# Three split fp32r passes for the transform matmuls of a long convolution, and a filter spectrum read once

## The chip, the cores and the metric

The kernel runs on one core of one Trainium2 chip. The metric is the device time of one execution in microseconds, lower is better. The core has a TensorE (PE, with its weight loads shown apart as PEld), a VectorE (DVE), a ScalarE (ACT), a GpSimd (POOL) and a SyncE (SP), which here issues nearly all of the DMAs. Each engine works through its own queue of instructions in order.

## The reference, cut to what matters

One encoder layer of 2048 positions by 1024 channels: a combined input projection, a Hyena group (512 channels, two gated long convolutions) beside an mLSTM group, an output projection, cross-attention, a squared-ReLU MLP and norms. The change touches the long convolution only:

```python
for o, gate in enumerate((g1, g2)):
    conv = irfft(rfft(z, n=2 * L) * spec[:, o], n=2 * L)[:, :L]
    z = gate * (conv + z * skip[o])
```

The spectrum `spec` is that of an implicit filter: a small sine network over position features, times a decay window, transformed in the same way. All inputs and outputs are fp32.

## The kernel before

**The transforms.** A transform of length 4096 over 2048 points is done as two matmul stages with constant matrices. The first stage multiplies slabs of 128x512 with the two 128x128 matrices `f1` (parity p = 0, 1); its result goes to DRAM and comes back regrouped; the second stage multiplies with one of 32 matrices `dm`. The inverse uses `em` and then `e2` in the same way. All of these are plain fp32 matmuls of 128x128 by 128x512.

**`filters`** (L158) makes the spectrum. For each of 16 slabs j and both orders o, it multiplies the hidden layer with `w3` (L253, L254), takes the window (DVE, L256 and L257), forms the sum (DVE, L261) and the difference (POOL, L262) of the forward and the backward part, and runs `front` (L238), which is the two `f1` matmuls, evicted by ScalarE (L239) into staging tiles that go to DRAM. A helper `late` holds back each `front` until the instructions of the next slab have been emitted. After that come 32 blocks of `dm` matmuls (L284), whose result is the spectrum `hd` in DRAM.

**`hyena`** (L627) has three stages for each order o. Stage one: per slab one load and two `f1` matmuls (L709), evicted by ScalarE and VectorE in turn (L140, L142). Middle stage, 16 steps: `load2` (L654) fetches `dm`, `em`, the regrouped slab `t` and the spectrum's real and imaginary rows `hr`, `hi`, each of them twice, once for partitions 0 to 63 and once for 64 to 127 (L664, L665); then for each of two halves the `dm` matmul (L723), two 64x512 instructions on ScalarE that swap the halves (L725, L726), a product on VectorE (L727), a product on POOL (L728), a sum on VectorE (L729), and, held back by one half, the `em` matmul (L691) with its eviction (L692) and the store `zg` (L694). Last stage: per slab two accumulating `e2` matmuls for each of two halves (L742) and the gate product (L743).

**The projection beside it.** `sweep` and `natural` (L495, L592) do the input projection. They already work with split operands: a helper writes a rounded high part in fp32r (ScalarE) and the rest as a low part (VectorE), and `mm3` (L294) runs three fp32r matmuls, high by high, high by low and low by high (L295 to L297).

**The order of the work.** `weave` interleaves `filters`, then `hyena`, with the projection's generators by the costs that they yield; the pools give the number of buffers (`a`: slabs of 128x1024, `b`: tiles of 128x512, and four PSUM banks under each of the tags `hy` and `mm`). Within what the program's order and the buffers allow, the framework orders the instructions of each engine by a modelled timeline, so a change in one place moves instructions on all engines.

In time, the span runs through `filters` with the projection (to about 470 us), `hyena` with the projection (to about 1130 us), then memory projection, mLSTM, output projection, attention and the MLP, which hold the rest.

Of the kernel before, what the change touches and what calls it, by code (L numbers as in the profile page):

```python
# [20 lines left out]
CH = 512  # L21
# [76 lines left out]
class Prog:  # L98
# [22 lines left out]
    def mm(self):  # L121
        return self.ps.tile([128, 512], F32, tag="mm", name="mm", bufs=4)
# [35 lines left out]
    def filters(self):  # L158
# [1 line left out]
        sd = [self.dram(f"fs{o}", (2, 128, 16, CH)) for o in range(2)]  # L160
        hd = self.dram("hd", (2, 32, 128, CH))
        with tc.tile_pool(name="f_sb", bufs=1, side="right") as sb:
            def ta(bufs=7):
                return sb.tile([128, 2, CH], F32, tag="a", name="a", bufs=bufs)

            def tb(bufs=8):
                return sb.tile([128, CH], F32, tag="b", name="b", bufs=bufs)

            w1 = sb.tile([66, 128], F32, name="w1")
            w2 = sb.tile([128, 128], F32, name="w2")  # L170
            w3 = sb.tile([128, 2, CH], F32, name="w3")
            f1 = sb.tile([128, 2, 128], F32, name="f1")
            nc.vector.memset(w1, 0.0)
            nc.vector.memset(w2, 0.0)
            nc.gpsimd.dma_start(out=w1[0:33, 0:64], in_=a["hy_filt_w1"][0])
# [8 lines left out]
            w3v = a["hy_filt_w3"][0].rearrange("k (o r c) -> r k o c", o=2, r=2)  # L184
            for h in range(2):
                nc.gpsimd.dma_start(out=w3[64 * h:64 * h + 64], in_=w3v[h])
            nc.gpsimd.dma_start(out=f1, in_=a["c_f1"])

            def sine(dst, src, b, fr):
                u, k = tb(), tb()  # L190
# [44 lines left out]
            def front(e, st, jj, o, js):  # L235
                for p in range(2):
                    pp = self.hy()
                    nc.tensor.matmul(pp, f1[:, p], e[p], start=True, stop=True)  # L238
                    nc.scalar.copy(st[p][:, jj], pp)  # L239
                    if jj == 1:  # L240
                        nc.sync.dma_start(out=sd[o][p, :, js], in_=st[p])

            nxt = windows(0)
            for j2 in range(8):
                js = slice(2 * j2, 2 * j2 + 2)
                yield 14
                (wf, wb), nxt = nxt, windows(j2 + 1)
                for o in range(2):
                    st = [ta() for p in range(2)]
                    for jj in range(2):  # L250
                        j = 2 * j2 + jj
                        pf, pb = self.hy(), self.hy()
                        nc.tensor.matmul(pf, hid[0:64, j::16], w3[0:64, o], start=True, stop=True)  # L253
                        nc.tensor.matmul(pb, hid[64:128, j::16], w3[64:128, o], start=True, stop=True)  # L254
                        f, b = tb(), tb()
                        nc.vector.tensor_tensor(f, pf, wf[:, jj], ALU.mult)  # L256
                        nc.vector.tensor_tensor(b, pb, wb[:, jj], ALU.mult)  # L257
                        if j == 0:
                            nc.vector.tensor_tensor(f[0:1], f[0:1], (skip, skip2)[o][0:1], ALU.add)
                        e = [tb() for p in range(2)]  # L260
                        nc.vector.tensor_tensor(e[0], f, b, ALU.add)  # L261
                        nc.gpsimd.tensor_tensor(e[1], f, b, ALU.subtract)  # L262
                        late(lambda e=e, st=st, jj=jj, o=o, js=js: front(e, st, jj, o, js))
            late(None)
            def blocks(o, i):
# [27 lines left out]
    def mm3(self, ps, lh, ll, rh, rl, start, stop):  # L293
        mm = self.nc.tensor.matmul  # L294
        mm(ps, lh, rh, start=start, stop=False)  # L295
        mm(ps, lh, rl, start=False, stop=False)  # L296
        mm(ps, ll, rh, start=False, stop=stop)  # L297

    def split(self, hi, lo, src):
        self.nc.scalar.copy(hi, src)  # L300
# [326 lines left out]
    def hyena(self, es):  # L627
# [7 lines left out]
        sb = es.enter_context(tc.tile_pool(name="h_sb", bufs=1, side="right"))  # L635

        def ta():
            return sb.tile([128, 2, CH], F32, tag="a", name="a", bufs=10)

        def tb():  # L640
            return sb.tile([128, CH], F32, tag="b", name="b", bufs=5)

        f1 = sb.tile([128, 2, 128], F32, name="f1")
        e2 = sb.tile([128, 2, 128], F32, name="e2")
        nc.sync.dma_start(out=f1, in_=a["c_f1"])
        nc.sync.dma_start(out=e2, in_=a["c_e2"])
        ghy = self.bcast(sb, a["hy_norm_g"], CH, "ghy")
        def load1(o, j2):
            z = ta()
# [4 lines left out]
        def load2(o, i):  # L654
            p, k = divmod(2 * i, 16)
            dm = sb.tile([128, 2, 128], F32, tag="dm", name="dm", bufs=2)
            em = sb.tile([128, 2, 128], F32, tag="em", name="em", bufs=2)
            nc.sync.dma_start(out=dm, in_=a["c_dm"][:, 2 * i:2 * i + 2])
            nc.sync.dma_start(out=em, in_=a["c_em"][:, 2 * i:2 * i + 2])
            t, hr, hi = ta(), ta(), ta()  # L660
            nc.sync.dma_start(out=t, in_=sds[o][p, 8 * k:8 * k + 16].rearrange("(k r) j c -> (r j) k c", k=2))
            src = hd[o, 2 * i:2 * i + 2].rearrange("k (r l) c -> r l k c", r=2)
            for h in range(2):
                nc.sync.dma_start(out=hr[64 * h:64 * h + 64], in_=src[0])  # L664
                nc.sync.dma_start(out=hi[64 * h:64 * h + 64], in_=src[1])  # L665
            if i == 0:
                nc.sync.dma_start(out=hr[64:65, 0], in_=hd[o, 0, 64:65])
                nc.vector.memset(hi[0:1, 0], 0.0)
                nc.vector.memset(hi[64:65, 0], 0.0)  # L669
            return dm, em, t, hr, hi  # L670
# [25 lines left out]
        for o in range(2):  # L696
            sd, gd = sds[o], gds[o]
            q = [load1(o, 0), load1(o, 1)]
            for j2 in range(8):
                yield 3.5  # L700
                js = slice(2 * j2, 2 * j2 + 2)
                z = q.pop(0)
                if j2 < 6:
                    q.append(load1(o, j2 + 2))
                st = [ta() for p in range(2)]
                for jj in range(2):
                    for p in range(2):
                        pp = self.hy()
                        nc.tensor.matmul(pp, f1[:, p], z[:, jj], start=True, stop=True)  # L709
                        self.copy(st[p][:, jj], pp)  # L710
                for p in range(2):
                    nc.sync.dma_start(out=sd[p, :, js], in_=st[p])
            nxt = load2(o, 0)
            for i in range(16):
                yield 3.5
                p, k = divmod(2 * i, 16)
                dm, em, t, hr, hi = nxt
                if i < 15:
                    nxt = load2(o, i + 1)
                gs = ta()  # L720
                for m in range(2):
                    pp = self.hy()
                    nc.tensor.matmul(pp, dm[:, m], t[:, m], start=True, stop=True)  # L723
                    xt, y = tb(), tb()
                    nc.scalar.activation(xt[0:64], pp[64:128], AF.Copy, scale=-1.0)  # L725
                    nc.scalar.copy(xt[64:128], pp[0:64])  # L726
                    nc.vector.tensor_tensor(y, pp, hr[:, m], ALU.mult)  # L727
                    nc.gpsimd.tensor_tensor(xt, xt, hi[:, m], ALU.mult)  # L728
                    nc.vector.tensor_tensor(y, y, xt, ALU.add)  # L729
                    late(lambda m=m, em=em, y=y, gs=gs, dst=gd[p, 8 * k:8 * k + 16]: back(m, em, y, gs, dst))  # L730
            late(None)
            nxt = load3(o, 0)
            for j2 in range(8):
                yield 3.5
                js = slice(2 * j2, 2 * j2 + 2)
                r, gate = nxt
                if j2 < 7:
                    nxt = load3(o, j2 + 1)
                for jj in range(2):
                    pp = self.hy()  # L740
                    for p in range(2):
                        nc.tensor.matmul(pp, e2[:, p], r[p][:, jj], start=p == 0, stop=p == 1)  # L742
# [922 lines left out]
```

## Time and profile before

| | |
|---|---|
| time, median of 3 runs | 3452.99 us (3443.19 to 3454.02) |
| time of the profiled execution | 3453.44 us |
| its span (first to last instruction) | 3451.7 us |
| mean granted clock of TensorE | 0.971 |
| TensorE busy | 3220.7 us (93%) |
| VectorE, ScalarE, GpSimd busy | 2116.4, 1256.9, 1274.5 us |
| DMA, mean over the span | 208 GB/s |

The profile is of one execution. Busy time of TensorE is modelled and pipelined: a matmul's recorded duration overlaps that of the next one, so throughput is read from start to start. A plain fp32 matmul leaves two records, an fp32r matmul one. An idle time is put down to the engine or DMA that released the waiting instruction.

### The profile page before, as it was taken

How to read it: one execution, taken by the hardware profiler on the slowest of the kernel's cores; microseconds unless marked ns; L12 is line 12 of the kernel's file. 1: busy time of each engine (PE TensorE's matmuls, PEld its weight loads, DVE VectorE, ACT ScalarE, POOL GpSimd, SP SyncE). 2: the span in 40 equal slices, each digit the busy share in tenths (PEclk: the TensorE clock that was granted, in tenths of full speed). 3: DMA queues.
4: the chain of work that ended last, by engine and by line, in shares of the span. 5: the costliest groups of instructions: out<-in, count | busy, mean ns of one | idle time of the engine just before them, and what ended most of it. 6: DMA issues, size and time to landing. Idle time of an engine off the chain costs nothing. (4 is left out here: it accounts for less than half of the span.)

```text
span 3451.7 us, 46201 instructions
## 1 busy us (share of the span) xinstructions
PE 3220.7 (93%) x15671; PEld 2574.5 (75%) x15671; DVE 2116.4 (61%) x3831; ACT 1256.9 (36%) x2410; POOL 1274.5 (37%) x902
## 2 busy tenths in 40 slices
PE   6999999999999888699998998999999988999997
PEld 5656666676666878598988896778788867888876
DVE  7585235434547667666865344888977734555695
ACT  4344435623553334323333333222322233333335
POOL 2131002200123212233334114776765577344483
PEclk9999999999999989799999999999999999999999
DMA  5356879987898589767767546665644465344434
GB/s 163 115 202 212 295 270 261 289 316 246 226 246 292 152 269 296 226 226 260 242 248 257 208 170 205 208 198 165 205 164 147 144 217 179 120 149 135 133 96 156
DMA packets 477704, 716.98 MB, mean 208 GB/s; under 512 B 41258, under 2 KB 259440, under 8 KB 468252
## 3 DMA queue, kind: packets, MB, share of 16 engines
q1 hardware_dynamic: 475864, 711.16, 64.4%
q0 software_dynamic: 1600, 2.86, 0.4%
q8 instruction: 124, 2.03, 0.2%
q14 instruction: 112, 0.92, 0.1%
q10 hardware_dynamic: 4, 0.00, 0.0%
HBM read 486.31 MB, written 227.57 MB: 207 GB/s over the span
## 5 line engine op out<-in xcount | busy, mean ns | idle before, releaser
L1273 DVE TENSOR_TENSOR bl<-wr,bh 128x512 fp32r<-128x512 f32 x213 | 229.0, 1079 | 201.6 <-ACT bh L1272 198.7
L295 PE MATMUL mm<-xh,wh 128*128 128x512 f32 (+1 forms) x768 | 316.8, 413 | 12.1 <-ACT P L531 7.1
L296 PE MATMUL mm<-xl,wh 128*128 128x512 f32 (+1 forms) x768 | 303.1, 395 | 0.3 <-DVE xr_y L150 0.2
L297 PE MATMUL mm<-xh,wl 128*128 128x512 f32 (+1 forms) x768 | 302.9, 395 | 0.6 <-DVE wl L301 0.6
L728 POOL TENSOR_TENSOR b<-b,a 128x512 f32<-128x512 f32 x64 | 90.3, 1412 | 497.0 <-DVE a L669 226.3
L1272 ACT CAST ah<-w 128x512 fp32r<-128x512 f32 x190 | 117.0, 622 | 380.5 <-PE mm L296 162.9
L301 DVE TENSOR_TENSOR wl<-wn,wh 128x512 fp32r<-128x512 f32 (+1 forms) x224 | 164.4, 762 | 137.2 <-ACT wh L300 136.6
L1272 ACT CAST bh<-wr 128x512 fp32r<-128x512 f32 x232 | 143.7, 620 | 272.6 <-PE mm L297 196.8
L297 PE MATMUL mm<-bh,al 128*128 128x512 f32 x576 | 222.6, 397 | 20.9 <-POOL al L1273 18.7
L295 PE MATMUL mm<-bh,ah 128*128 128x512 f32 x576 | 228.7, 397 | 7.4 <-ACT ah L1272 7.4
L296 PE MATMUL mm<-bl,ah 128*128 128x512 f32 x576 | 227.4, 395 | 0.0
L1273 DVE TENSOR_TENSOR al<-w,ah 128x512 fp32r<-128x512 f32 x190 | 188.5, 993 | 32.5 <-ACT ah L1272 32.1
L297 PE MATMUL mm<-act,wl 128*128 128x512 f32 x512 | 202.8, 399 | 4.1 <-DMA wl<-vw 4.1
L295 PE MATMUL mm<-act,wh 128*128 128x512 f32 x512 | 201.8, 398 | 2.5 <-DMA wh<-vw 2.5
L296 PE MATMUL mm<-act,wh 128*128 128x512 f32 x512 | 202.7, 396 | 0.0
L300 ACT CAST wh<-wn 128x512 fp32r<-128x512 f32 (+1 forms) x224 | 130.3, 619 | 192.7 <-PE mm L296 75.3
L295 PEld LDWEIGHTS mm<-xh,wh 128*128 128x128 f32 x768 | 148.8, 194 | 60.9 <-issue 18.2
L1141 POOL TENSOR_TENSOR ssum<-ssum,sq 128x512 f32<-128x512 f32 x56 | 75.8, 1354 | 309.7 <-ACT sq L1140 305.2
L296 PEld LDWEIGHTS mm<-xl,wh 128*128 128x128 f32 x768 | 148.8, 194 | 45.2 <-issue 19.5
L297 PEld LDWEIGHTS mm<-xh,wl 128*128 128x128 f32 x768 | 148.6, 193 | 42.9 <-issue 15.8
L295 PE MATMUL hy<-bh,ah 128*128 128x512 f32 x448 | 175.5, 392 | 3.0 <-DVE acc L1544 3.0
L296 PE MATMUL hy<-bl,ah 128*128 128x512 f32 x448 | 174.6, 390 | 0.0
(371 smaller groups left out, 9094.2 us busy)
## 6 DMA issues: line engine op xcount, KB each, us to landing
wr<-hc SPq DMA_DIRECT2D x224, 256.0 KB
a<-hd SPq DMA_DIRECT2D x128, 256.0 KB
w<-in_ff_w_dram SPq DMA_DIRECT2D x128, 256.0 KB
hc<-t SPq DMA_DIRECT2D x128, 256.0 KB
wn<-in_w_in_dram SPq DMA_DIRECT2D x104, 256.0 KB
hc<-q SPq DMA_DIRECT2D x96, 256.0 KB
fs<-a SPq DMA_DIRECT2D x32, 512.0 KB
a<-fs SPq DMA_DIRECT2D x32, 512.0 KB
```

Source lines behind the costliest of these rows:

```text
L295: mm(ps, lh, rh, start=start, stop=False)
L296: mm(ps, lh, rl, start=False, stop=False)
L297: mm(ps, ll, rh, start=False, stop=stop)
L300: self.nc.scalar.copy(hi, src)
L301: self.nc.vector.tensor_tensor(lo, src, hi.bitcast(F32), ALU.subtract)
L728: nc.gpsimd.tensor_tensor(xt, xt, hi[:, m], ALU.mult)
L1141: nc.gpsimd.tensor_tensor(ssum, ssum, sq, ALU.add)
L1272: self.nc.scalar.copy(hi, src)
L1273: eng.tensor_tensor(lo, src, hi.bitcast(F32), ALU.subtract)
```

## The change

Three matmul groups, those at L238 (`front`), L709 and L742, become three split passes each with `mm3`. Their constant matrices are split once into a high and a low part; the moving tiles are split where they are used by a new helper `halved`: a cast on ScalarE and a subtraction on VectorE or POOL. The matmuls with `dm`, `em`, `w1`, `w2` and `w3` stay plain fp32. In `load2`, each spectrum row is loaded once, into one half of the partitions, and copied to the other half by ScalarE. The pools change: in `filters` `a` from 7 to 6 buffers and `b` from 8 to 10, in `hyena` `a` from 10 to 9 and `b` from 5 to 7.

```diff
@@ filters
-                nc.tensor.matmul(pp, f1[:, p], e[p], start=True, stop=True)
+                self.mm3(pp, f1[0][:, p], f1[1][:, p], *e[p], True, True)
...
                         nc.vector.tensor_tensor(e[0], f, b, ALU.add)
                         nc.gpsimd.tensor_tensor(e[1], f, b, ALU.subtract)
+                        e = [self.halved(sb, e[p], (nc.vector, nc.gpsimd)[p], tag="b", name="b", bufs=10) for p in range(2)]
@@ new helper
+    def halved(self, pool, src, eng, **kw):
+        hi, lo = (pool.tile(list(src.shape), F32R, **(kw or {"name": n})) for n in ("ch", "cl"))
+        self.nc.scalar.copy(hi, src)
+        eng.tensor_tensor(lo, src, hi.bitcast(F32), ALU.subtract)
+        return hi, lo
@@ hyena, load2
-            for h in range(2):
-                nc.sync.dma_start(out=hr[64 * h:64 * h + 64], in_=src[0])
-                nc.sync.dma_start(out=hi[64 * h:64 * h + 64], in_=src[1])
+            nc.sync.dma_start(out=hr[0:64], in_=src[0])
+            nc.sync.dma_start(out=hi[64:128], in_=src[1])
+            nc.scalar.copy(hr[64:128], hr[0:64])
+            nc.scalar.copy(hi[0:64], hi[64:128])
@@ hyena, stage one
+                    zh, zl = self.halved(sb, z[:, jj], nc.vector, tag="b", name="b", bufs=7)
                     for p in range(2):
                         pp = self.hy()
-                        nc.tensor.matmul(pp, f1[:, p], z[:, jj], start=True, stop=True)
+                        self.mm3(pp, f1[0][:, p], f1[1][:, p], zh, zl, True, True)
@@ hyena, last stage
-                        nc.tensor.matmul(pp, e2[:, p], r[p][:, jj], start=p == 0, stop=p == 1)
+                        rh, rl = self.halved(sb, r[p][:, jj], (nc.vector, nc.gpsimd)[p], tag="b", name="b", bufs=7)
+                        self.mm3(pp, e2[0][:, p], e2[1][:, p], rh, rl, p == 0, p == 1)
```

More of the change, by code (lines that the diff above doesn't have):

```diff
@@ L162, in filters, with ta, tb @@
         with tc.tile_pool(name="f_sb", bufs=1, side="right") as sb:
-            def ta(bufs=7):
+            def ta(bufs=6):
                 return sb.tile([128, 2, CH], F32, tag="a", name="a", bufs=bufs)
-            def tb(bufs=8):
+            def tb(bufs=10):
                 return sb.tile([128, CH], F32, tag="b", name="b", bufs=bufs)
@@ L171, in filters @@
             w3 = sb.tile([128, 2, CH], F32, name="w3")
-            f1 = sb.tile([128, 2, 128], F32, name="f1")
             nc.vector.memset(w1, 0.0)
@@ L186, in filters @@
                 nc.gpsimd.dma_start(out=w3[64 * h:64 * h + 64], in_=w3v[h])
-            nc.gpsimd.dma_start(out=f1, in_=a["c_f1"])
+            t = tb()[:, 0:256].rearrange("p (a b) -> p a b", a=2)
+            nc.gpsimd.dma_start(out=t, in_=a["c_f1"])
+            f1 = self.halved(sb, t, nc.vector)
             def sine(dst, src, b, fr):
@@ L637, in ta @@
         def ta():
-            return sb.tile([128, 2, CH], F32, tag="a", name="a", bufs=10)
+            return sb.tile([128, 2, CH], F32, tag="a", name="a", bufs=9)
         def tb():
[L641 to L646, printed above, removed]
+            return sb.tile([128, CH], F32, tag="b", name="b", bufs=7)
+        consts = []
+        for n in ("c_f1", "c_e2"):
+            t = ta()[:, 0, 0:256].rearrange("p (a b) -> p a b", a=2)
+            nc.sync.dma_start(out=t, in_=a[n])
+            h, l = (sb.tile([128, 2, 128], F32R, name=n + x) for x in "hl")
+            nc.scalar.copy(h, t)
+            nc.vector.tensor_tensor(l, t, h.bitcast(F32), ALU.subtract)
+            consts.append((h, l))
+        f1, e2 = consts
         ghy = self.bcast(sb, a["hy_norm_g"], CH, "ghy")
```

## The prediction

> **What bounds the kernel now.** First I read the page's busy line, then busy time by stretch, cut where the convolution's stages change. A stretch row gives its length, then busy time of PE, PEld, DVE, ACT and POOL, the granted clock, DMA share and GB/s.
>
> ```profile
> PE 3220.7 (93%) x15671; PEld 2574.5 (75%) x15671; DVE 2116.4 (61%) x3831; ACT 1256.9 (36%) x2410; POOL 1274.5 (37%) x902
> ...
> 105.00:310.00 205.00, 203.18 (x711) 119.09 (x710) 143.22 (x283) 81.88 (x155) 58.48 (x32) 1.00 0.49 168
> 310.00:470.00 160.00, 157.69 (x628) 109.45 (x627) 41.19 (x59) 69.15 (x118) 0.59 (x1) 1.00 0.85 282
> 470.00:550.00 80.00, 77.13 (x299) 51.06 (x299) 30.25 (x49) 29.21 (x47) 4.27 (x3) 1.00 0.80 254
> 550.00:720.00 170.00, 159.10 (x691) 113.80 (x690) 90.80 (x157) 97.55 (x163) 38.73 (x30) 0.98 1.01 283
> 720.00:850.00 130.00, 126.66 (x717) 94.86 (x715) 46.07 (x110) 34.68 (x78) 0.00 (x0) 1.00 0.78 288
> 850.00:1050.00 200.00, 183.84 (x706) 126.53 (x707) 104.75 (x170) 105.91 (x174) 46.01 (x31) 0.97 0.93 242
> 1050.00:1130.00 80.00, 77.41 (x386) 57.63 (x385) 64.09 (x152) 21.37 (x39) 30.41 (x20) 0.98 0.83 278
> ```
>
> TensorE is the bound nearly everywhere: 203 of 205 us in the filters' first part, and 281 of 290 us in the three stretches that hold most of hyena's stage one and last stage (470–550, 720–850, 1050–1130). Only the two middle stretches are looser: PE leaves 11 and 16 us, 27 in all, while the DMA share is 1.01 and 0.93. So fewer TensorE cycles are worth having there, if nothing new holds TensorE up. What holds it today in hyena, and what the middle stage's other engines wait for:
>
> ```profile
> PE hy L691 <- DVE b L729: 9.4, 5, 3.3
> PE mm L295 <- ACT P L531: 4.2, 1, 4.2
> PE hy L691 <- ACT P L531: 3.8, 1, 3.8
> PE hy L723 <- DMA a<-zs: 3.5, 3, 2.3
> ...
> L727 DVE TENSOR_TENSOR b<-hy,a 128x512 f32<-128x512 f32 x64 | 44.1, 688 | 80.4 <-ACT b L726 40.5 <-DMA a<-hd 29.9 <-ACT a L692 5.4
> L728 POOL TENSOR_TENSOR b<-b,a 128x512 f32<-128x512 f32 x64 | 90.3, 1412 | 497.0 <-DVE a L669 226.3 <-ACT b L726 197.0 <-DMA a<-hd 39.0
> ```
>
> The largest wait is for the middle stage's chain, which ends in the sum L729, and that chain is itself late because the spectrum (`hd`) lands late: 29.9 us of waiting on DVE, 39.0 on POOL.
>
> **The matmuls.** Durations overlap, so I count from start to start.
>
> ```profile
> 1033.75 0.39 PE L296 MATMUL mm<-xl,wh 128*128 128x512 f32 x1
> ...
> 1037.23 0.39 PE L296 MATMUL mm<-xl,wh 128*128 128x512 f32 x1
> 1037.46 1.02 PE L691 MATMUL hy<-b,em 128*128 128x512 f32 x2
> 1038.32 1.02 PE L723 MATMUL hy<-a,dm 128*128 128x512 f32 x2
> ...
> L238 PE MATMUL hy<-b,f 128*128 128x512 f32 x128 | 64.4, 607 | 0.2 <-DVE ms L408 0.2
> L709 PE MATMUL hy<-a,f 128*128 128x512 f32 x128 | 61.0, 593 | 1.7 <-DMA a<-hy 1.7
> L742 PE MATMUL hy<-a,e 128*128 128x512 f32 x128 | 59.4, 592 | 0.0
> ```
>
> Fifteen split passes, each with weights of its own, lie between 1033.75 and 1037.23: 0.232 us a pass, 0.70 for three. One plain fp32 matmul of this shape takes 1037.46 to 1038.32, 0.86 us, in two records. Each of the three lines has 128 records, so 64 matmuls: 192 x (0.86 - 0.70) = 31 us of TensorE come off, 10 at L238 and 10.5 each at L709 and L742. By recorded durations it would be a loss (three of 0.39 against two of 0.59 is a wash); I take the starts, since those are what the next instruction sees.
>
> [...]
>
> **Hyena's stage one and last stage.** They add 32 + 64 splits: a cast on ScalarE and a subtraction each, 64 of these on DVE and 32 on POOL. Nearest rows:
>
> ```profile
> L300 ACT CAST wh<-wn 128x512 fp32r<-128x512 f32 x56 | 31.9, 617 | 52.1 <-DMA wn<-in_w_in_dram 36.8 <-PE mm L296 9.8 <-PE mm L297 5.3
> L301 DVE TENSOR_TENSOR wl<-wn,wh 128x512 fp32r<-128x512 f32 x53 | 36.3, 714 | 51.8 <-ACT wh L300 51.8
> L1273 POOL TENSOR_TENSOR al<-wr,ah 128x512 fp32r<-128x512 f32 x52 | 70.5, 1361 | 97.7 <-ACT ah L1272 92.0 <-issue 5.7
> ```
>
> ACT 96 x 0.62 = 59 us, DVE 64 x 0.71 = 46, POOL 32 x 1.36 = 44. The three stretches have 290 us, of which ACT works 85, DVE 140 and POOL 35, and the slabs are loaded one or two ahead, so the splits lie beside TensorE's work. Uncovered, one split ahead of its matmul would cost 0.62 + 0.71 (DVE) to 1.36 us (POOL). Of 21 us I take 18 as won (PE is busy 97% there).
>
> **Filters.** They add 64 splits: ACT 40 us on 82 of 205, DVE 32 subtractions on 143, POOL 32 on 58. Totals fit, so the question is the chain.
>
> ```profile
> 195.81 0.80 PE L253 MATMUL hy<-w,hid 64*128 64x512 f32 x1
> ...
> 198.89 0.80 PE L253 MATMUL hy<-w,hid 64*128 64x512 f32 x1
> ...
> L256 DVE TENSOR_TENSOR b<-hy,a 128x512 f32<-128x512 f32 x32 | 22.0, 686 | 22.2 <-PE hy L253 12.7 <-PE hy L254 9.2
> L262 POOL TENSOR_TENSOR b<-b 128x512 f32<-128x512 f32 x32 | 58.5, 1828 | 223.1 <-DVE b L257 186.8 <-DVE xr_y L155 8.7 <-DVE xr_t L153 8.0
> ```
>
> Where slabs follow each other with no projection between them, one takes 3.08 us (195.81 to 198.89). From the `w3` matmuls to `front` lie two window products (2 x 0.69) and POOL's difference (1.83): 3.2 us. After the change the POOL half adds a cast (0.62) and a second POOL instruction (1.83): 5.7 us. `late` puts one `front` (2 x 0.70) and one pair of `w3` matmuls (1.36, that is 3.08 less two fp32 matmuls of 0.86) between; the loop over two slabs then takes 5.7 + 1.4 + 1.36 = 8.5, 4.2 per slab in place of 3.1. So a slab without projection work beside it loses 1.1 us, and one with it wins its share of 10 us. All 32 dense: 35 lost. I take a third, 11 slabs, as in such runs: 12 lost, 10 won, **+2 us**; bounds -10 and +25. Staging in 6 buffers in place of 7 makes an eviction wait for the store of the slab before; that is inside these bounds.
>
> **The middle stage.** Half of the spectrum's loads go, and 64 copies of 64x1024 come to ScalarE. The spectrum's share of the traffic, over 550 to 700 us:
>
> ```profile
> DMA packets 29598, 43.01 MB, mean 287 GB/s; under 512 B 2737, under 2 KB 14608, under 8 KB 29589
> ...
> a<-hd SPq DMA_DIRECT2D x54, 256.0 KB
> ...
> L726 ACT COPY b<-hy 64x512 f32<-64x512 f32 x64 | 37.0, 578 | 0.8
> L545 ACT ACTIVATE cv<-P,cb,cw 128x1040 f32<-128x1040 f32 x12 | 15.1, 1256 | 0.4
> ```
>
> 54 x 0.256 = 13.8 of 43.0 MB; half is 6.9 MB, 16% of the traffic at a share of 1.01, and two issues fewer per step on SP. For the copy the trace shows no row; a crossing copy of half the width takes 0.58 (L726) and a full-width instruction of 1040 elements 1.26, so 0.58 to 1.26; I take 1.15, near the row of equal length. 64 x 1.15 = 74 us raise ACT from 203 to 277 of the 370 us. ScalarE is in order: in the changed build the pair stands in most steps straight ahead of the half-swap of the next half, and behind a copy that waits for its load are queued that swap, the evictions L692 and the projection's PSUM copies, for which TensorE waits (4.2 and 3.8 us above). DMA relief is worth at most TensorE's 27 idle us; exposed copies at most 74. I take **-7**: the waits for `hd` shrink, and a part is given back.
>
> Small edits cost nothing that can be seen: the three constants are split once, beside the projection's matmuls, under 5 us if uncovered (three casts and subtractions of less than 0.62 + 0.71). At step 0 of each order the one-row load into `hr` now waits for ScalarE's copy, and SP's later loads stand behind it: twice a copy, 2.5 us at most, and loads run a step ahead.
>
> **Sum**: -18 + 2 - 7 = -23 us. The profiled execution took 3453.44 us (span 3451.7 and 1.7 around it), 0.45 above the median of the runs; 3453.4 - 23 = 3430 us. About 0.3%, 10 us, is what a measurement of this kernel can tell from no change. What follows after 1130 us keeps its work; its instructions are reordered in places, for which I leave some us in the range.
>
> **Rivals.**
> - *Relief pays too* (0.17): all 31 us are kept and 18 of the 27 idle us go: 3404. For it: share 1.01 and the waits for `hd`. Against it: ACT at 75%.
> - *The filters' chain eats it* (0.18): every slab is exposed, +35 - 10 = +25 cancels -18 - 7: 3453. For it: DVE at 143 of 205, and POOL's instruction takes 1.83 there against 1.36 elsewhere, so the two engines already slow each other and now both get 32 more. Against it: PE is busy 203 of 205 us there, so projection passes lie between most slabs. [...]
> - *ScalarE holds up the middle stage* (0.23): half of the 74 us stays uncovered, because the copies and their wait for the load stand ahead of the half-swap: -18 + 2 + 37 = +21, 3474, slower. It beats the gain from 16 us, 0.5 us a step over 32 steps, and shows from 0.8. For it: L691 already waits for this chain, and a late load, which today stops DVE or POOL, would stop ScalarE. Against it: fewer bytes land sooner, and TensorE has projection passes between.
>
> **How the numbers follow.** The forecast has 0.42, by itself 3418 to 3443. Faster by over 0.3%: forecast and relief, 0.59. Within: 0.18. Slower: 0.23. The range, 3400 to 3476, takes in the rivals' values and leaves out full exposure of the copies and full relief.
>
> **What would show it.** Per triple of the new matmuls 0.70 from start to start; less than 3 us between the splits and their matmuls as PE idle in 470–550 and 720–850; the end of the last stage near 1107 in place of 1130. In the middle stage, DMA share near 0.85 and waits for `hd` on ACT under 20 us; a PE idle time over 40 us there, released by ACT or L729, means the third rival. In the filters, PE idle before `front` released by POOL above 25 us means the second. A triple at 0.86 or more would refute the whole saving.

## The result and the profile after

| | before | after |
|---|---|---|
| time, median of 4 runs each | 3453.51 us (3443.19 to 3454.84) | 3473.47 us (3470.0 to 3475.6) |
| ratio after to before, 95% interval | | 1.0065 [1.0049, 1.0081] |
| time and span of the profiled execution | 3453.44, 3451.7 us | 3474.58, 3472.9 us |
| mean granted clock of TensorE | 0.971 | 0.964 |
| first and last `dm` matmul of the filters start at | 313.5, 459.7 us | 349.0, 486.9 us |
| last `em` matmul of the middle stage starts at | 1056.8 us | 1084.7 us |

The kernel became 20 us slower, where 23 us faster was forecast. The page's busy line, of the kernel after:

```profile
PE 3229.6 (93%) x15863; PEld 2622.7 (76%) x15863; DVE 2200.2 (63%) x3930; ACT 1399.9 (40%) x2628; POOL 1359.8 (39%) x966
```

TensorE's modelled busy time is 9 us longer, although it has 31 us less to do by start-to-start prices. So here instructions took longer each, or were held inside what is counted as busy. The stretch rows of the kernel after, cut at its own stage ends (length; busy time of PE, PEld, DVE, ACT, POOL; granted clock, DMA share, GB/s), say where:

```profile
105.00:350.00 245.00, 238.33 (x836) 151.67 (x835) 178.31 (x317) 118.26 (x223) 101.13 (x64) 0.91 0.42 144
350.00:480.00 130.00, 128.27 (x502) 87.00 (x500) 32.30 (x48) 58.57 (x101) 0.00 (x0) 1.00 0.95 321
480.00:580.00 100.00, 94.98 (x414) 74.48 (x413) 50.50 (x78) 54.00 (x86) 3.13 (x3) 0.97 0.67 218
580.00:750.00 170.00, 154.77 (x684) 111.70 (x683) 85.88 (x153) 123.63 (x190) 40.45 (x30) 0.98 0.81 237
...
870.00:1090.00 220.00, 204.02 (x810) 144.44 (x809) 114.06 (x194) 144.97 (x219) 42.47 (x32) 0.98 0.68 193
1090.00:1190.00 100.00, 85.56 (x575) 78.48 (x574) 93.36 (x183) 40.38 (x78) 55.52 (x37) 0.97 0.67 222
```

The filters' first part took 205 us before (105 to 310, granted clock 1.00) and takes 245 now, at a clock of 0.91. From there on the delay of 27 us of the last filter `dm` matmul is carried along (28 us at the last `em`). The middle stage (580 to 750 and 870 to 1090) has the load relief: DMA shares of 0.81 and 0.68 where 1.01 and 0.93 stood. The last row is hyena's last stage in the second order: VectorE works 93 of 100 us and TensorE 86, where TensorE worked 77 of 80.

**What happens in the filters.** The same kernel in slices of 5 us, columns as above:

```profile
180.00:185.00 5.00, 4.76 (x27) 3.33 (x26) 5.00 (x6) 4.58 (x9) 3.23 (x2) 1.00 0.44 127
185.00:190.00 5.00, 2.78 (x7) 0.98 (x6) 5.00 (x13) 4.80 (x13) 1.28 (x2) 1.00 0.61 238
190.00:195.00 5.00, 4.97 (x8) 1.83 (x8) 4.98 (x21) 1.73 (x4) 2.90 (x2) 0.53 0.66 230
195.00:200.00 5.00, 5.00 (x8) 2.17 (x8) 5.00 (x12) 1.49 (x3) 1.26 (x1) 0.50 0.09 34
200.00:205.00 5.00, 5.00 (x17) 3.27 (x16) 3.70 (x6) 2.71 (x5) 3.07 (x2) 0.61 0.32 126
...
235.00:240.00 5.00, 4.37 (x8) 1.62 (x7) 5.00 (x17) 1.50 (x3) 2.94 (x2) 0.81 0.26 105
240.00:245.00 5.00, 4.54 (x15) 3.46 (x15) 5.00 (x10) 2.43 (x5) 2.31 (x3) 0.51 0.11 13
...
265.00:270.00 5.00, 3.21 (x7) 1.40 (x7) 3.31 (x7) 4.23 (x12) 2.33 (x2) 0.88 0.20 57
270.00:275.00 5.00, 5.00 (x9) 2.00 (x9) 5.00 (x17) 2.10 (x4) 2.37 (x3) 0.50 0.53 211
...
285.00:290.00 5.00, 5.00 (x15) 2.85 (x14) 2.08 (x3) 2.28 (x4) 0.00 (x0) 0.50 0.50 174
```

Read two columns together. In 185 to 190 TensorE is busy 2.78 of 5 us; in the next ten microseconds it counts as busy throughout, at half the clock. The same follows the gap at 265, and, with less idle time ahead of it, it happens at 235. Cut into slices of half a microsecond and less, the same view puts the half clock at 190.3 to 203.9, 238.1 to 244.9 and 268.8 to 292.7 us: 13.7, 6.8 and 23.9 us. A busy digit of 9 hides most of this; only the clock column shows it. The timeline of all engines over that first gap (start, duration, then what waited and for whom), same kernel:

```profile
186.59 1.87 DVE L309 TENSOR_TENSOR xl<-mm,xh 128x512 fp32r<-128x512 f32 x3
...
186.72 1.23 PE L255 MATMUL hy<-w,hid 64*128 64x512 f32 x2 [0.32 <-DVE b L258]
...
188.47 0.68 DVE L262 TENSOR_TENSOR b<-b 128x512 f32<-128x512 f32 x1
...
189.18 1.14 ACT L303 CAST b<-b 128x512 fp32r<-128x512 f32 x2 [0.20 <-DVE b L262]
...
189.85 1.31 PE L297 MATMUL hy<-b,ch 128*128 128x512 f32 x2 [1.90 <-ACT b L303]
190.19 0.69 DVE L304 TENSOR_TENSOR b<-b 128x512 fp32r<-128x512 f32 x1
...
190.96 0.77 PE L298 MATMUL hy<-b,ch 128*128 128x512 f32 x1
191.53 0.63 PE L299 MATMUL hy<-b,cl 128*128 128x512 f32 x1
192.09 2.07 PE L254 MATMUL hy<-w,hid 64*128 64x512 f32 x2
```

The chain is one of three engines, on queues that have other work: VectorE's sum (L262) stands behind three of the projection's own subtractions (L309), ScalarE's cast (L303) waits 0.20 us for the sum, TensorE waits 1.90 us for the cast, and then the clock is gone: the pair of `w3` matmuls takes 2.07 us where it took 1.23.

Counted in sum: the last filter `dm` matmul is 27 us late although the stage was relieved of 10 us, so 37 us were lost; by then both kernels have done the same work of the projection (283 split triples before, 285 after). The clock accounts for 0.09 x 245 = 22 of them. Of the other 15 the busy rows show 5 as idle time (238.33 of 245 busy, against 203.18 of 205); where the last 10 lie isn't shown.

The saving per triple is there where the clock is full (1.00 from 261.5 to 263). The middle pass (L298) of two triples that follow each other, kernel after:

```profile
261.91 0.39 PE L298 MATMUL hy<-b,ch 128*128 128x512 f32 x1
...
262.61 0.39 PE L298 MATMUL hy<-b,ch 128*128 128x512 f32 x1
```

0.70 us from start to start, as forecast.

### The profile page after: what moved, and what is told of

Its sections match the earlier page's. It is cut to its first block, busy times and chain, and to the rows that moved or that the text cites. A ratio compares the mean times of both kernels' runs of the same rounds, so it can differ in the third digit from the quotient of the medians.

```text
span 3472.9 us, 46975 instructions
## 1 busy us (share of the span) xinstructions
PE 3229.6 (93%) x15863; PEld 2622.7 (76%) x15863; DVE 2200.2 (63%) x3930; ACT 1399.9 (40%) x2628; POOL 1359.8 (39%) x966
## 3 DMA queue, kind: packets, MB, share of 16 engines
q0 software_dynamic: 1600, 2.86, 0.4%
## 5 line engine op out<-in xcount | busy, mean ns | idle before, releaser
L297 PE MATMUL mm<-xh,wh 128*128 128x512 f32 (+1 forms) x768 | 307.8, 402 | 22.6 <-DVE st L142 9.2
L298 PE MATMUL mm<-xl,wh 128*128 128x512 f32 (+1 forms) x768 | 304.9, 397 | 0.0
L298 PE MATMUL mm<-bl,ah 128*128 128x512 f32 x576 | 228.1, 396 | 0.0
L309 DVE TENSOR_TENSOR wl<-wn,wh 128x512 fp32r<-128x512 f32 (+1 forms) x224 | 171.7, 795 | 84.6 <-ACT wh L308 84.0
L298 PE MATMUL mm<-act,wh 128*128 128x512 f32 x512 | 202.9, 396 | 0.0
L298 PEld LDWEIGHTS mm<-xl,wh 128*128 128x128 f32 x768 | 150.1, 195 | 41.7 <-issue 15.6
L298 PE MATMUL hy<-bl,ah 128*128 128x512 f32 x448 | 175.8, 393 | 0.0
```

The lines of the kernel that those rows point to most:

```text
L309: self.nc.vector.tensor_tensor(lo, src, hi.bitcast(F32), ALU.subtract)
```

## The experiments

Ratios are to the kernel before, run beside each group of experiments on the same chip; its median moved between 3443 and 3451 us from group to group, so ratios are compared, not times. "Filters alone" and the like mean the kernel before with that one edit.

| label | what it is | median us | ratio [95%] |
|---|---|---|---|
| e1_filters_as_before | after, filters as before | 3452.64 | 1.0006 [0.9994, 1.0019] |
| e2_filters_alone | filters alone | 3483.06 | 1.0091 [1.0068, 1.0113] |
| e3_load_alone | `load2` alone | 3453.14 | 1.0010 [0.9997, 1.0024] |
| e4_stages_alone | split stage one and last stage alone | 3453.99 | 1.0014 [0.9996, 1.0032] |
| e5_low_on_vector | e2, both low parts on VectorE | 3469.29 | 1.0055 [1.0038, 1.0073] |
| e6_no_low | e2 without the low parts | 3442.07 | 0.9959 [0.9943, 0.9976] |
| e7_no_low_8_tiles | e6 with 8 `b` tiles | 3438.56 | 0.9966 [0.9953, 0.9980] |
| e8_last_stage_plain_in_second_order | e4, last stage of the second order plain | 3446.33 | 0.9990 [0.9975, 1.0005] |
| e9_both_loads_and_copies | all loads kept, copies added | 3474.36 | 1.0062 [1.0042, 1.0081] |
| e10_filters_with_filler | e2 with idle TensorE work added | 3469.84 | 1.0051 [1.0031, 1.0072] |
| e11_stages_less_last_with_load | e8 and `load2` | 3441.26 | 0.9966 [0.9950, 0.9982] |
| e12_stage_one_alone | split stage one alone | 3446.92 | 0.9992 [0.9975, 1.0010] |
| e13_load_copies_on_gpsimd | e3, copies on GpSimd | 3428.17 | 0.9956 [0.9943, 0.9969] |
| e14_e11_copies_on_gpsimd | e11, copies on GpSimd | 3415.79 | 0.9923 [0.9895, 0.9951] |
| e15_e11_copies_on_vector | e11, copies on VectorE | 3416.44 | 0.9923 [0.9899, 0.9948] |
| e16_load_copies_on_vector | e3, copies on VectorE | 3419.65 | 0.9935 [0.9914, 0.9956] |

### The three parts, each by itself

The first four take the change apart: `filters` as before and all else as after (e1), and each part on the kernel before (e2, e3, e4). No other line is edited, and the pools go with their part.

> The changed kernel with the filters' part put back as it was before (plain fp32 front, 7 and 8 buffers); hyena's three edits stay. Theory F (the filters' longer chain costs about 38 us, from TensorE work counted start to start: 68 us lost between 105 and 350 us against 30 between 105 and 310 before): 3473 less 28 (38 lost there less 10 saved), about 3440 to 3447, faster than before. Theory S (ScalarE's copies, which wait 79 us for the spectrum's load, hold up the middle stage): stays at 3465 or above, since the middle stage is unchanged.

> The kernel before with the filters' edit alone. Theory F: 3453 + 28 = about 3480, slower than the whole change. Theory S: 3443, the 10 us of saved TensorE time, or no change.

> The kernel before with load2's edit alone (each spectrum row loaded once and copied by ScalarE), buffers as before. Theory F: within 8 us of 3453 either way, since TensorE lost 45 us in the two middle stretches of the changed kernel and 43 before. Theory S: 3475 to 3490, the waits of the copies reach TensorE.

> The kernel before with the split passes of hyena's stage one and last stage alone (9 and 7 buffers), loads as before. Prediction's term: 3453 - 18 = 3435. Rival (the last stage of the second order becomes bound by VectorE, 93 of 100 us busy in the changed kernel): 3445 to 3450, most of the 21 us given back.

The filters alone cost 0.91%, 31 us; without them nothing is lost (1.0006). e2 and e3 came where theory F had them; e1 came 6 us above its range and e4 4 us above its rival's, each far from the other theory. Neither of the other two parts brings anything: the 21 us of TensorE time that leave stage one and the last stage come to nothing, and so does the relief from half of the spectrum's traffic. The filters' loss is the one seen in the kernel after; e2's row for the same stretch:

```profile
105.00:350.00 245.00, 238.35 (x838) 151.77 (x836) 178.49 (x317) 118.00 (x223) 101.25 (x64) 0.91 0.42 144
```

Same busy times, same clock of 0.91, with the load and the stages left as before. Beside the other parts the filters' edit costs 20 us (after against e1) and alone 31; why some 10 us are won back there wasn't settled.

### The filters: casts, subtractions, slots or the clock

Four edits on top of e2. In e5 GpSimd's subtraction goes to VectorE. Theory P, here and in the two runs after it, is that GpSimd's second instruction, in series behind its difference, makes the chain long (for e5: 3455 to 3465):

```diff
-  e = [self.halved(sb, e[p], (nc.vector, nc.gpsimd)[p], tag="b", name="b", bufs=10) for p in range(2)]
+  e = [self.halved(sb, e[p], nc.vector, tag="b", name="b", bufs=10) for p in range(2)]
```

> The kernel before with the filters' edit alone, but both low parts subtracted by VectorE, so that GpSimd has one instruction per slab again. Measured for the edit as it is: 3483, 33 over the kernel before. [...] Theory D (VectorE is the tight engine there, some 80% busy in 150 to 250 us): slower still, 3490. Theory T (tile slots hold the chain): no change, about 3483.

In e6 the casts stay and the subtractions go; the pass with the low part takes the high part again, so that TensorE's work is unchanged and the correction for the moving operand is left out. e7 is the same with 8 `b` tiles in place of 10.

```diff
-  e = [self.halved(sb, e[p], (nc.vector, nc.gpsimd)[p], tag="b", name="b", bufs=10) for p in range(2)]
+  for p in range(2):
+      hi = sb.tile([128, CH], F32R, tag="b", name="b", bufs=10)
+      nc.scalar.copy(hi, e[p])
+      e[p] = hi, hi
```

> The filters' edit alone without the low part of the moving tiles: the second pass takes the high part again, so the result misses that correction; three passes, casts on ScalarE, no subtraction, six tile slots used per slab in place of eight. Theories P and D (the subtractions): below 3450, about 3443, the saved TensorE time. Theory A (ScalarE's casts in the chain): stays above 3465.

> As the run without the low part (same work left out), but with 8 slots in the pool for six tiles per slab, as tight as 10 for eight. Theory T (tile slots hold the chain): above 3465, most of the loss is back. Theories P and D: as without the low part, within 8 us of it.

Without the subtractions, but with all the casts, the edit is a gain of 0.41% (0.34% with 8 tiles): 14 and 12 us, the forecast's 10 us of saved TensorE time and a little more. In the filters themselves less than that shows: the first filter `dm` matmul starts at 309.3 and 307.7 us, against 313.5 before (349.2 in e2); where the rest was won isn't shown. So the casts cost nothing that counts, and the slots neither. The subtractions cost 0.91 + 0.41 = 1.3%, 45 us, between e2 and e6. With the second one on VectorE (e5) 0.36% comes back, 12 us. None of the three theories was met: P had two thirds of the loss coming back, D had it growing, T had no change. So the loss isn't GpSimd's slow instruction alone. What came back is clock: 0.96 over 105 to 350 us where e2 has 0.91, 12 us of full-speed time. What the instructions take in the kernel after, from the groups by line (busy, mean ns | idle before, releaser):

```profile
L263 POOL TENSOR_TENSOR b<-b 128x512 f32<-128x512 f32 x32 | 56.4, 1764 | 154.4 <-DVE b L258 141.3 <-DVE xr_y L155 5.7 <-DVE P L534 2.3
...
L304 POOL TENSOR_TENSOR b<-b 128x512 fp32r<-128x512 f32 x32 | 44.8, 1399 | 65.7 <-ACT b L303 65.7
...
L303 ACT CAST b<-b 128x512 fp32r<-128x512 f32 x64 | 39.1, 621 | 43.4 <-DVE b L262 31.3 <-POOL b L263 5.1 <-DVE P L534 3.6
...
L262 DVE TENSOR_TENSOR b<-b 128x512 f32<-128x512 f32 x32 | 31.2, 976 | 0.4
...
L304 DVE TENSOR_TENSOR b<-b 128x512 fp32r<-128x512 f32 x32 | 25.1, 784 | 16.6 <-ACT b L303 15.3 <-POOL b L263 1.2
```

The casts wait for VectorE's sum (31.3 us) far more than for GpSimd's difference (5.1): VectorE is the late one. Its sum has no idle time before it (0.4) because other work always stands ahead of it. And it takes longer than before, 0.98 us on the mean in place of 0.79. Single slabs show why (timeline of the kernel after):

```profile
192.28 1.26 POOL L263 TENSOR_TENSOR b<-b 128x512 f32<-128x512 f32 x1 [0.25 <-DVE xr_t L153]
192.30 1.78 DVE L262 TENSOR_TENSOR b<-b 128x512 f32<-128x512 f32 x1
...
301.15 0.69 DVE L262 TENSOR_TENSOR b<-b 128x512 f32<-128x512 f32 x1
301.19 1.80 POOL L263 TENSOR_TENSOR b<-b 128x512 f32<-128x512 f32 x1 [3.96 <-DVE b L258]
```

In 14 of the 32 slabs the sum starts first; it then takes 0.68 to 0.80 us, and the difference 1.73 to 1.81. In ten the difference starts first and the sum ends 0.55 us after it, which makes it 1.13 to 1.81 us long; in the other eight the sum is short (0.67 to 0.79). So one holds up the other. The kernel before has three long sums, and e5, where GpSimd has no subtraction, has four.

How much of the loss is the clock was asked with e10: four extra passes of 256 columns ahead of each triple, whose result the triple overwrites. In its trace such a pass takes 0.119 us from start to start (the median), so this is 64 x 4 x 0.119 = 30 us of work, where 33 had been reckoned.

```diff
   for p in range(2):
       pp = self.hy()
+      for _ in range(4):
+          nc.tensor.matmul(pp[:, 0:256], f1[0][:, p], warm, start=True, stop=True)
       self.mm3(pp, f1[0][:, p], f1[1][:, p], *e[p], True, True)
```

> The kernel before with the filters' edit alone, and four extra passes of 256 columns ahead of each triple of front, whose result the triple overwrites: 64 x 4 x 0.127 = 33 us more TensorE work, which can run while TensorE waits for the splits and keeps it busy. The filters' edit alone measured 3483, and its granted clock fell to 0.76 to 0.91 between 150 and 300 us. Theory C (the fall of the clock after such waits makes most of the loss): clock back to 0.97 or more there, and no slower than 3483, down to 3465. Theory W (the waits themselves make the loss, the clock little): 3490 to 3515.

30 us more work and 0.40%, 14 us, less time than e2, as theory C had it; the first filter `dm` matmul starts at 335.8 us, 13 us earlier than in e2. Beside e2's row above, the same stretch of e10:

```profile
105.00:350.00 245.00, 239.01 (x1102) 172.24 (x1101) 181.81 (x317) 121.47 (x228) 99.92 (x64) 0.97 0.46 161
```

and of e6, which has no subtractions:

```profile
105.00:350.00 245.00, 237.52 (x953) 160.41 (x952) 153.31 (x299) 134.62 (x251) 55.34 (x32) 0.99 0.57 195
```

The clock is 0.97 with the filler and 0.99 without the subtractions, against 0.91: 15 and 20 us of full-speed time over 245. The filler is done in time that the chain would have left empty, and the clock stays at 0.97. That the chain comes first and the clock's fall adds to it is shown by e6 and e10 together; how the 14 us divide isn't shown, since the filler also shifts the order of other work.

### The load: two large effects that cancel

e9 keeps all four loads of a step and adds the two ScalarE copies, which then rewrite what was loaded:

```diff
             for h in range(2):
                 nc.sync.dma_start(out=hr[64 * h:64 * h + 64], in_=src[0])
                 nc.sync.dma_start(out=hi[64 * h:64 * h + 64], in_=src[1])
+            nc.scalar.copy(hr[64:128], hr[0:64])
+            nc.scalar.copy(hi[0:64], hi[64:128])
```

> The kernel before, with both loads of each spectrum row kept and ScalarE's copies added on top (they write the same values again): the price of the copies without the relief of the loads. The load edit alone measured 3453 against 3450. Theory N (both are worth nothing, TensorE is not held up by either): 3450 to 3456. Theory X (the two cancel): the copies alone cost 10 to 30, 3460 to 3480.

The copies alone cost 0.62%, 21 us, and the missing loads give 0.52%, 18 us, back (e3 against e9). This is not quite the copies' price in the change: in e9 a copy also waits for the load that it overwrites, 100 us in all for the first of each pair, where e3 has 82. e13 and e16 keep the relief and take the copies to another engine, for instance

```diff
-            nc.scalar.copy(hr[64:128], hr[0:64])
-            nc.scalar.copy(hi[0:64], hi[64:128])
+            nc.gpsimd.tensor_copy(hr[64:128], hr[0:64])
+            nc.gpsimd.tensor_copy(hi[0:64], hi[64:128])
```

> The kernel before with the load edit alone, the copies on GpSimd in place of ScalarE. On ScalarE they cost 24 us (both loads and copies: 3474) and the halved loads gave about 21 back (3453). Theory Q (the price is that of ScalarE's queue: swap and evictions stand behind a copy that waits for its load): GpSimd has only the product there, so the relief comes through, 3432 to 3442. Theory L (the price is the copy's own time between load and product, wherever it runs, and GpSimd's copy is no shorter): 3450 to 3465.

> The kernel before with the load edit alone, copies on VectorE. Theory Q: 3450 to 3460. Theory L: 3450 to 3460 if the copy takes about 1 us as on ScalarE, below 3445 if it is clearly shorter.

Gains of 0.44% and 0.65%, 15 and 22 us. The forecasts start from 3450 us, so these ratios stand for 3435 and 3428. On GpSimd theory Q was met and theory L is out: its copy is no shorter than ScalarE's (1.11 us against 1.05), and the relief comes through. For VectorE theory Q stood at 3450 to 3460 and missed by 22 us, while theory L's case of a clearly shorter copy, below 3445, was met (0.76 us against 1.05). Of each kernel, the copy of `hr` and the eviction of the `em` matmul (groups by line; idle before, and who ended it). First the kernel before, which has no copy:

```profile
L692 ACT COPY a<-hy 128x512 f32<-128x512 f32 x64 | 37.3, 583 | 49.0 <-PE hy L691 48.0 <-DMA kt<-cv 0.6
```

The same groups of e3, copies on ScalarE:

```profile
L671 ACT COPY a<-a 64x1024 f32<-64x1024 f32 x32 | 33.4, 1045 | 81.7 <-DMA a<-hd 81.6
...
L699 ACT COPY a<-hy 128x512 f32<-128x512 f32 x64 | 37.2, 580 | 7.5 <-PE hy L698 7.2
```

of e13, copies on GpSimd:

```profile
L671 POOL COPY a<-a 64x1024 f32<-64x1024 f32 x32 | 35.6, 1114 | 303.5 <-DMA a<-hd 229.4 <-DMA hy<-st 68.5 <-issue 5.6
...
L699 ACT COPY a<-hy 128x512 f32<-128x512 f32 x64 | 37.3, 583 | 54.5 <-PE hy L698 46.8 <-POOL a L672 3.7 <-issue 3.2
```

and of e16, copies on VectorE:

```profile
L671 DVE COPY a<-a 64x1024 f32<-64x1024 f32 x32 | 24.4, 761 | 59.2 <-DMA a<-hd 58.7
...
L699 ACT COPY a<-hy 128x512 f32<-128x512 f32 x64 | 37.3, 583 | 51.4 <-PE hy L698 48.7 <-issue 2.6
```

Read the eviction's idle time. Before, ScalarE stood ready and waited 48 us for the `em` matmuls: it was early. With the copies on ScalarE the engine stands 82 us in front of a load that hasn't landed, and at the eviction it waits only 7 us: it has become late, and what it evicts is late. With the copies elsewhere it is early again (47 and 49 us), although GpSimd then waits 229 us for the same load. So a wait of 229 us is cheaper than one of 82; what differs is what stands behind it in the queue. The stretch row of 550 to 720 shows it for the first order's middle stage; e3:

```profile
550.00:720.00 170.00, 150.63 (x613) 104.33 (x612) 85.43 (x147) 120.99 (x183) 41.58 (x29) 0.96 0.75 217
```

e9, which has the copies and all the loads:

```profile
550.00:720.00 170.00, 151.59 (x614) 105.30 (x614) 83.79 (x148) 118.77 (x179) 36.95 (x28) 0.96 0.93 252
```

e13:

```profile
550.00:720.00 170.00, 165.52 (x805) 124.21 (x804) 97.61 (x155) 98.42 (x167) 74.03 (x57) 1.00 0.79 232
```

and e16:

```profile
550.00:720.00 170.00, 163.39 (x736) 117.44 (x735) 111.73 (x184) 97.21 (x163) 42.30 (x29) 1.00 0.83 255
```

TensorE leaves 18 to 19 us with the copies on ScalarE, whether the loads are halved or not, and 4 to 7 with the copies elsewhere; before it was 11. In the second order (850 to 1050) it leaves 14 in e3, 24 in e9, and 6 to 8 with the copies elsewhere, against 16 before. And ScalarE was never full: 121 of 170 us. VectorE does the copy in 0.76 us, ScalarE in 1.05, GpSimd in 1.11 to 1.18. Why VectorE, which also has the chain's product and sum behind the copy, does better than GpSimd is not settled; the shorter copy is one candidate, and no run separates it from the order of the queues.

### Stage one and the last stage: where 21 us went

e8 leaves the last stage of the second order plain, and e12 the last stage of both; the rest is e4.

```diff
                     for p in range(2):
+                        if o:
+                            nc.tensor.matmul(pp, e2f[:, p], r[p][:, jj], start=p == 0, stop=p == 1)
+                            continue
                         rh, rl = self.halved(sb, r[p][:, jj], (nc.vector, nc.gpsimd)[p], tag="b", name="b", bufs=7)
```

> The kernel before with the split passes in hyena's stage one and in the last stage of the first order; the last stage of the second order stays plain fp32. The stages alone measured 3454 against 3450, so 21 us of TensorE time gave nothing. Theory V (the splits of the last stage meet a full VectorE in the second order, where the group norm runs): 3450 - 16 = 3434 to 3440. Rival (the freed TensorE time is lost wherever it falls, in waits for DMA in the middle stage): 3448 to 3454.

> Split passes in hyena's stage one alone, 10.5 us of TensorE time. Theory V (only the last stage's splits meet a full VectorE): 3440. Rival (freed TensorE time in stage one is lost again in the middle stage, where DMA share is 1.0): 3447 to 3452.

16 us of TensorE time less in e8 and 10.5 less in e12 give 0.10% and 0.08%, with intervals that hold no change. Theory V is met by neither; e12 stands at the edge of its rival's range, e8 between the two. Taking away the split of the second order's last stage is worth 0.24% (e4 against e8, intervals that overlap), so that part alone may cost some 8 us in place of winning 5. For e4, the stretches that answer to the quoted ones of before:

```profile
470.00:550.00 80.00, 75.68 (x348) 60.20 (x347) 41.29 (x66) 37.70 (x63) 2.58 (x2) 1.00 0.79 254
550.00:720.00 170.00, 154.75 (x641) 108.08 (x641) 85.76 (x154) 97.05 (x163) 38.76 (x30) 0.95 1.03 270
720.00:850.00 130.00, 122.44 (x798) 109.15 (x797) 65.97 (x128) 61.68 (x125) 21.72 (x16) 0.97 0.89 312
850.00:1050.00 200.00, 188.85 (x756) 134.31 (x755) 111.72 (x187) 110.27 (x183) 45.80 (x32) 0.99 0.92 247
...
1100.00:1150.00 50.00, 42.41 (x254) 38.97 (x255) 48.64 (x95) 11.81 (x24) 31.31 (x21) 0.86 0.59 192
```

and the longest wait of its TensorE between 1050 and 1190 us (in total, times, longest):

```profile
PE hy L296 <- DVE b L302: 10.0, 4, 3.5
```

In the last stretch VectorE works 48.64 of 50 us, TensorE waits for its subtraction (L302), and the granted clock is 0.86. From 1050 to 1200 these 16 subtractions take 1.04 us each, with GpSimd's beside them, where e12's take 0.69. That stretch before:

```profile
1100.00:1150.00 50.00, 47.86 (x324) 40.93 (x322) 44.91 (x108) 8.47 (x24) 24.44 (x16) 1.00 0.62 199
```

VectorE was already at 90% there (the norm after the gate product), which a row cut at 1130 hid. Over 470 to 850, e4 leaves 27.1 us of TensorE idle against 17.1 before, and its clock costs 0.05 x 170 + 0.03 x 130 = 12 us against 0.02 x 170 = 3: the freed time reappears as idle time and as clock. That is an account of where it is, not of why; for the last stage the wait names the cause, for stage one none was found. Two leads have no run. In e4, e8 and e12 TensorE waits 6.3, 7.5 and 8.9 us for the projection's `xn` on VectorE between 470 and 1150 us, against 0.7 before. And all three carry the change's pools in `hyena` (9 slabs `a` in place of 10), which no run has by themselves.

### A version that beats both

e11 is e8 with the `load2` of the change; e14 and e15 have its copies on GpSimd and on VectorE, as above. All three keep the filters of before.

> Split passes in hyena's stage one and in the last stage of the first order only, and the load edit; filters as before. If the load's relief lets the freed 16 us of TensorE through (waits for the regrouped slab and the spectrum in the middle stage): 3435 to 3442. If not: as without the load edit, 3444 to 3450.

> Split passes in stage one and the last stage of the first order, and the load edit with its copies on GpSimd; with them on ScalarE it measured 3441. Theory Q: 3420 to 3430, a version that beats both kernels by more. Theory L: 3440 to 3455.

> The same with the copies on VectorE. Theory Q: VectorE also has the product and the sum of the chain and the projection's subtractions behind them, so it costs as on ScalarE, 3440 to 3455. Theory L: the same range, unless VectorE copies in well under 1 us, then below 3438.

e14 takes 3415.79 us, 0.77% [0.49 to 1.05] less than before, as theory Q had it (0.9923 x 3450 = 3423). e11 gains 0.34% with the copies on ScalarE, where e8 and e3 alone gain next to nothing, so there the parts don't add up as if they were independent. With the copies elsewhere that isn't clear: on GpSimd the stages add 0.33% to the load's gain (e14 against e13), within the intervals, on VectorE 0.12% (e15 against e16), about what e8 gives alone. The stretch row of e14 in the middle stage:

```profile
850.00:1050.00 200.00, 198.24 (x822) 142.07 (x821) 112.67 (x152) 114.78 (x178) 81.38 (x61) 1.00 0.73 221
```

TensorE is busy 198 of 200 us at a clock of 1.00, where 184 at 0.97 stood before. e15 does as well; theory Q had 3440 to 3455 for it, by the same reasoning that missed e16, and theory L's case of a short copy, below 3438, was met again (0.84 and 0.79 us).

## Why the prediction was wrong, point by point

**"Filters +2", bounds -10 and +25: the step that failed.** Alone the part costs 31 us. The prediction sized the chain as GpSimd's (a difference and a second instruction of 1.83 us each; the second took 1.40) and the exposure as a third of the slabs. The runs show the chain on VectorE first (the casts wait 31.3 us for its sum, 5.1 for GpSimd's difference), where the subtraction stands in one queue with the projection's work, and show a second price that the sum didn't have: at three places, after waits of which the longest were 1.90, 0.45 and 1.49 us, TensorE's clock falls to 0.50 for 7 to 24 us (22 of the 37 us lost). "PE is busy 203 of 205 us there, so projection passes lie between most slabs" was the wrong inference: over 185 to 190 there were none, nor at the other two places, and three such places made the 22 us. The check named for this, over 25 us of waits released by GpSimd, wasn't met either: TensorE's waits in that part are short, the largest sum is 4.3 us for ScalarE's cast, GpSimd releases none of 0.2 us or more, and most of the loss that can be placed sits in the clock.

What exactly brings the clock down and back isn't shown: the longest waits ahead of the three falls were 1.90, 0.45 and 1.49 us, the stretches at 0.50 that followed lasted 13.7, 6.8 and 23.9, and from 270 to 290 the clock stayed at 0.50 with TensorE counted busy for 19.75 of 20 us. The 1.83 the prediction read rightly, as VectorE and GpSimd slowing each other. Here, in ten slabs, the sum is held up by a difference that started first (1.78 us in the one shown), and of the two differences shown the one behind a sum takes 1.80 and the one ahead of a sum 1.26. The longer sums take some 9 us more of VectorE's time than 32 of 0.69 would (an estimate from the mean of 0.98); how much of the loss they set off no run separates from the queues.

**"Stages one and last -18": failed.** Measured +5 (e4), -3 for stage one alone (e12), both within the noise. 0.70 per triple came out there too, so the saving was real and the step "I take 18 as won (PE is busy 97% there)" was what failed: a stretch in which TensorE is busy 97% didn't pass the saving on where VectorE, at 90% in the second order, got 16 more instructions. That is the last stage's part; why stage one's saving didn't come through stays open.

**"The middle stage -7": right in size, wrong in its terms.** Measured +3 (e3, not different from nothing): +21 for the copies and -18 for the loads. The copy took 1.05 us (1.15 was taken), and DMA share fell as forecast (0.81 and 0.68). "Waits for `hd` on ACT under 20 us" was wrong; the group of the first copy in the kernel after:

```profile
L678 ACT COPY a<-a 64x1024 f32<-64x1024 f32 x32 | 33.5, 1046 | 78.9 <-DMA a<-hd 78.7
```

They came to 79 us. The price of a copy was not its 1.05 us but the load that it waits for, in ScalarE's queue: one starts at 629.50 after a wait of 4.29 us, and the eviction of an `em` matmul that had started at 624.91 (1.02 us) comes behind both copies, at 631.72.

**The rivals.** "ScalarE holds up the middle stage" forecast 3474, and 3473 was measured, by luck and not by its way: with the ScalarE copies in place and the filters as before the time is 3453 (e1), and its sign, over 40 us of TensorE idle in the middle stage, didn't come (31). Its mechanism is real (e9, e13) and was paid for by the loads. "The filters' chain eats it" named the right place. Its 35 us lost is near the 37 counted above by luck: it took them as 1.1 us from each of 32 slabs, and more than half of them are the clock at three places. "Relief pays too" is what e14 comes nearest to, once neither filters nor ScalarE stand against it: 27 us less, where it forecast 49.

**Cases and range.** The measured time lies in the range. The terms were added as if they were independent, and they aren't (alone they measure +31, +5 and +3, together +20). All three erred to the same side, and for two of them the reason is the same: in the filters and in the last stage the question was whether the engines' totals fit, where it should have been what stands in VectorE's queue ahead of the next matmul.

## What to carry to other kernels

When TensorE is the bound and a change hands work to other engines to relieve it, price the chain up to the next matmul at its barest place, where no other matmuls lie beside it, and not by the engine's share of the stage; and look at the granted clock in slices of a few microseconds, since here a wait of 1.90 us was followed by 13.7 us at a clock of 0.50. An instruction that waits for a transfer is worth trying on another engine's queue, even one where it takes as long and waits longer: here 64 copies of 1.05 us on ScalarE cost 21 us, and the same copies on GpSimd, waiting nearly three times as long, gave the relief of the halved loads. Parts that measure nothing each may do so because two effects cancel, so it pays to take away one of the two before a part is dropped.

## What the runs showed of the hardware that was not expected

- Waits of at most 1.90, 0.45 and 1.49 us on TensorE were followed by 13.7, 6.8 and 23.9 us at a granted clock of 0.50, nearly all of it counted as busy in the first and the last (4.75 to 5.00 of 5 us); passes of 0.23 us then start 0.43 us apart.
- 30 us of added matmuls made a kernel 14 us faster, its mean clock in that stretch rising from 0.91 to 0.97.
- A copy of 64x1024 across partition halves took 0.75 to 0.84 us on VectorE, 1.05 on ScalarE and 1.11 to 1.22 on GpSimd (e3, e13 to e16).
- In the kernel after, VectorE's sum of two tiles took 0.68 to 0.80 us where it started ahead of GpSimd's difference of the same tiles, and up to 1.81 where it started behind; the difference took 1.73 to 1.81 behind the sum, and 1.26 to 2.86 where it started first. On the mean the sum went from 0.79 us (before) to 0.98 (L262), the difference from 1.83 to 1.76.
